# State space of a two-layer hybrid model: blocks of 32 partitions change places by ScalarE copies in place of products with columns of the identity

## The chip, the cores and the metric

The kernel runs on one core of a Trainium2 chip, one launch for the whole model. The metric is the device time of one execution in microseconds (us). The engines that matter here are TensorE (PE in the rows; PEld is its weight load), VectorE (DVE), ScalarE (ACT), and SyncE (SP), whose queue issues the weight transfers. Matrix products end in PSUM, eight banks of 2 KB per partition; all else lies in SBUF, on 128 partitions.

## The reference, cut to what matters

Two layers, 256 tokens, width 1024. Each layer adds a gated mixer of three branches (attention, state space, convolution) and then a feed-forward part: dense in layer 0, eight experts with two chosen per token in layer 1.

```python
for layer in range(2):
    h = rmsnorm(x, norm_mix[layer])
    z = h @ w_in[layer]
    cq, ckv, kpe, u_ssm, conv_a, conv_g, gates = split(z)
    y_attn = mla_branch(cq, ckv, kpe, ...) @ w_o_attn[layer]
    s = s5_branch(u_ssm, ...)
    s = gelu(s)
    s = s * sigmoid(s @ ssm_w_glu[layer] + ssm_b_glu[layer])
    y_ssm = s @ w_o_ssm[layer]
    y_conv = conformer_conv_branch(conv_a, conv_g, ...) @ w_o_conv[layer]
    g = sigmoid(gates).reshape(B, L, 3, D)
    x = x + (g[:, :, 0] * y_attn + g[:, :, 1] * y_ssm + g[:, :, 2] * y_conv) @ w_out[layer]
    x = x + (swiglu if layer == 0 else moe_swiglu)(rmsnorm(x, norm_ffn[layer]), ...)
return rmsnorm(x, norm_final)

# s5_branch, for each of 32 groups of 16 channels with 64 complex states:
#   state[t] = a * state[t-1] + B u[t];   y[t] = Re(C state[t]) + d * u[t]
```

The state space is 512 channels wide: 32 groups of 16.

## The kernel before

The whole is one program whose instructions a scheduler orders on PE, ACT, DVE and SP by their dependencies and buffers, starting from the order in which the program emits them. A plan per layer lists the weight pieces of the mixer ("u0", "gate4", "conv1", ...); after each piece the "lanes", generators such as the state space's `ssm_gen`, are advanced by a budget of estimated microseconds. Those estimates are the numbers that the lanes yield. So the state space's small steps lie between the products of the projections, and a step that becomes ready late delays whatever stands behind it on the same engine.

**Projections.** A weight piece of 128x1024 arrives in fp32. ACT writes its rounded high part (`bwh`, L198), DVE the remainder (`bwl`, L199), and PE makes three products of high and low parts per tile (L211 to L213, helper `mm3`). Three pairs of `bwh`/`bwl` buffers are in turn. In layer 0 the product with `ssm_w_glu` is made in plain fp32 instead (L209).

**State space.** `u`, the branch's input, holds channels on partitions and tokens along the row: four tiles of 128 channels x 256 tokens. The scan goes in steps of Q = 4 tokens, so that a sequence is NQ = 64 blocks of 4. For this, `U` holds, for each of 16 pairs of groups, 32 channels times 4 time steps on the 128 partitions and 64 blocks along the row. The work is done in two halves h of 8 pairs each:

- `states(h)` brings `u` to `U`: 16 products per half (4 blocks of 32 channels r, 4 steps st; L1225), each with 32 columns of the identity as weights and `tile_position` set, take partitions 32r.. of `u`, every fourth token, to partitions 32(3-st).. of a PSUM tile `aux`. ACT copies the bank to `U` (L1228, 128x512). 16 fp32 products with `minT` (L1232) then give `bu`.
- `turn_in`, `scans`, `turn_out` are DVE work: rotate by the tables `E`, 16 scans of 64 (L1270), rotate back into `P0` and `P1` (`hr`, `hi`), which have one buffer each.
- `out(h)` makes 8 times three products into the one `y` bank (L1241 with `toep` and `U`; L1242 with `mout` and `P0`; L1243 with `P1`), and ACT copies the bank to `ys` (L1245, 128x512).
- `ssm_act(h)` brings `ys` back to channels on partitions by 16 products per half with identity columns (L1315, into `aux`); DVE adds d times `u` (two instructions through the helper at L136, which read `aux` with a stride of 64 elements). ACT squares (L1322), DVE combines, ACT takes the tanh (L1324), DVE writes the gelu into `u`; then comes the product with `ssm_w_glu`, in layer 1 after a split of `u` into `br` (L201, L202).

The mixer's PSUM tiles are `mm` (two banks), `bu` (two), and one each of `aux`, `y`, `sc` and `o`. `aux` also serves attention's norms and transposes and the convolution's norm. An fp32 product runs through PE in two passes, so 16 products show as x32 in the trace.

Of the kernel before, what the change touches and what calls it, by code (L numbers as in the profile page):

```python
# [8 lines left out]
F32 = mybir.dt.float32  # L9
F32R = mybir.dt.float32r  # L10
I32 = mybir.dt.int32
AF = mybir.ActivationFunctionType
OP = mybir.AluOpType
# [10 lines left out]
Q = 4  # L24
NQ = L // Q
# [33 lines left out]
def pair_at(c):  # L59

    h, r, q = c // 8, c // 2 % 4, c % 2
    return 4 * (2 * h + q) + r
# [19 lines left out]
class Prog:  # L82
# [43 lines left out]
    def tt(self, out, a, b, op):  # L126
        self.nc.vector.tensor_tensor(out, a, b, op=op)
# [743 lines left out]
    def mixer(self, l, wk, psp, raw=None):  # L871
        nc, io = self.nc, self.io
# [18 lines left out]
        aux = lambda: psp.tile([128, 512], F32, name="aux", bufs=1)  # L891
# [64 lines left out]
        u = wk.tile([128, 4, L], F32, name="u", bufs=1)  # L956
# [5 lines left out]
        def pair(user):  # L962

            t = wk.tile([128, 2, 4, L], F32R, name="br", bufs=2)
            return (t[:, 0].bitcast(F32), None) if user in nat else (t[:, 0], t[:, 1])
# [247 lines left out]
        def ssm_gen():  # L1213
            E = self.E
            U = wk.tile([128, NCH, NQ], F32, name="U", bufs=1)
            wt = lambda nm: wk.tile([128, 8, NQ], F32, tag=nm, name=nm, bufs=1)

            def states(h):

                p = aux()  # L1220
                us = u[:, 2 * h:2 * h + 2].rearrange("p q (k s) -> p s q k", s=Q)
                for r in range(4):
                    for st in range(Q):
                        o = 32 * (Q - 1 - st)
                        nc.tensor.matmul(p[o:o + 32, r * 128:(r + 1) * 128],  # L1225
                                         self.ident[:, 32 * r:32 * r + 32], us[:, st],
                                         start=True, stop=True, tile_position=(0, o))
                nc.scalar.activation(U[:, 8 * h:8 * h + 8].rearrange("p a b -> p (a b)"), p, AF.Copy)  # L1228
                pb = psp.tile([128, 2, 8, NQ], F32, name="bu", bufs=1)
                for i in range(2):  # L1230
                    for c in range(8):
                        nc.tensor.matmul(pb[:, i, c], self.minT[i][:, pair_at(8 * h + c)], U[:, 8 * h + c],  # L1232
                                         start=True, stop=True)
                return pb

            def out(h, hr, hi):
                y = psp.tile([128, 8, NQ], F32, name="y", bufs=1)
                mo = lambda i, c: self.mout[i][:, pair_at(c)].rearrange("p k g o -> p (k g o)")
                for j in range(8):
                    c = 8 * h + j  # L1240
                    nc.tensor.matmul(y[:, j], self.toep[:, pair_at(c)], U[:, c], start=True, stop=False)  # L1241
                    nc.tensor.matmul(y[:, j, 1:], mo(0, c), hr[:, j, :NQ - 1], start=False, stop=False)  # L1242
                    nc.tensor.matmul(y[:, j, 1:], mo(1, c), hi[:, j, :NQ - 1], start=False, stop=True)  # L1243
                Y = wk.tile([128, 8, NQ], F32, tag="ys", name="ys", bufs=1)
                nc.scalar.activation(Y, y, AF.Copy)  # L1245
                return Y

            tt = lambda o, x, y, op: self.tt(o, x, y, op)

            def turn_in(h, pb, wr, wi):  # L1250

                pr, pi = pb[:, 0], pb[:, 1]
                C, S = (E[:, i, 8 * h:8 * h + 8] for i in range(2))
                t = wt("T0")
                tt(wr, pr, C, OP.mult)
                tt(t, pi, S, OP.mult)
                yield 1.2
                tt(wr, wr, t, OP.add)
                t = wt("T0")
                tt(wi, pi, C, OP.mult)  # L1260
                yield 1.2
                tt(t, pr, S, OP.mult)
                tt(wi, wi, t, OP.subtract)
                yield 1.2

            def scans(h, wr, wi):
                for w_ in (wr, wi):
                    for c in range(8):
                        k = 16 * l + pair_at(8 * h + c)
                        nc.vector.tensor_tensor_scan(w_[:, c], self.magq[:, k:k + 1].to_broadcast([128, NQ]), w_[:, c],  # L1270
                                                     0.0, op0=OP.mult, op1=OP.add)
                    yield 1.1

            def turn_out(h, wr, wi):

                C, S = (E[:, i, 8 * h:8 * h + 8] for i in range(2))
                hr, hi, t = wt("P0"), wt("P1"), wt("T0")
                tt(hr, wr, C, OP.mult)
                tt(t, wi, S, OP.mult)
                yield 1.2  # L1280
                tt(hr, hr, t, OP.subtract)
                tt(hi, wr, S, OP.mult)
                yield 1.2
                tt(wi, wi, C, OP.mult)
                tt(hi, hi, wi, OP.add)
                yield 1.2
                return out(h, hr, hi)

            w = [wt("wr"), wt("wi")]
            pb = states(0)  # L1290
            yield 0
            yield from turn_in(0, pb, *w)
            pb = states(1)
            sg["states"] = True
            yield from scans(0, *w)
            Y = yield from turn_out(0, *w)
            w = [wt("wr"), wt("wi")]
            yield from turn_in(1, pb, *w)
            ssm_act(0, Y)
            yield 2.2  # L1300
            yield from scans(1, *w)
            Y = yield from turn_out(1, *w)
            yield 0
            ssm_act(1, Y)
            yield 2.2

        def ssm_act(h, Y):

            if h == 0:
                sg["H"], sg["L"] = pair("glu")  # L1310
            p = aux()
            pv = p.rearrange("p (q s k) -> p q s k", q=2, s=Q)
            for r in range(4):
                for st in range(Q):
                    nc.tensor.matmul(pv[32 * r:32 * r + 32, :, st], self.ident[:, 32 * st:32 * st + 32],  # L1315
                                     Y[:, 2 * r:2 * r + 2], start=True, stop=True, tile_position=(0, 32 * r))
            for q in range(2):
                yv = u[:, 2 * h + q].rearrange("p (k s) -> p k s", s=Q)
                self.stt(yv, yv, self.f("ssm_d", l, 2 * h + q), pv[:, q].rearrange("p s k -> p k s"), OP.mult, OP.add)
            y = u[:, 2 * h:2 * h + 2].rearrange("p a b -> p (a b)")  # L1320
            t = wk.tile([128, 512], F32, tag="T1", name="lt", bufs=1)
            nc.scalar.activation(t, y, AF.Square, scale=math.sqrt(0.044715))  # L1322
            self.stt(t, t, 1.0, y, OP.add, OP.mult)
            nc.scalar.activation(t, t, AF.Tanh, scale=math.sqrt(2.0 / math.pi))  # L1324
            self.stt(y, t, 1.0, y, OP.add, OP.mult)
            if sg["L"] is not None:
                fl = lambda v: v[:, 2 * h:2 * h + 2].rearrange("p a b -> p (a b)")
                self.split(fl(sg["H"]), fl(sg["L"]), y, scale=0.5)
# [25 lines left out]
        if l == 0:  # L1354
            self.conv_params(psp)
        lanes = dict(tables=lambda: self.ssm_tables(l), out=lambda: self.ssm_out(l, psp),
                     norm=attn_norm, attn=attn_gen, ssm=ssm_gen, cln=conv_ln)
        lanes["in"] = lambda: self.ssm_inp(l, psp)
        needs = dict(ssm=("tables", "out", "in"), attn=("norm",), cln=("conv0", "conv1"))
        needs["in"] = ("out", "attn") if l == 0 else ()  # L1360
        for tok in self.plan[l]:
# [6 lines left out]
            name, i = t[:-1], int(t[-1], 16)  # L1368
# [621 lines left out]
```

## Time and profile before

| | |
|---|---|
| time, median of 3 runs | 1738.11 us (1738.04 to 1740.32) |
| the profiled execution's own time | 1739.71 us |
| its span in the profile | 1738.0 us |
| PE busy | 1696.0 us (98%) |
| DVE busy | 1473.3 us (85%) |
| ACT busy | 1164.1 us (67%) |
| chain that ended last | PE 92%, DVE 4%, ACT 2%, issue 1%, DMA 1% |
| mean granted TensorE clock | 0.992 |

The span is first to last instruction. The granted clock is the share of TensorE's full speed that the chip allowed. Layer 0's mixer lies in about the first 200 us of the span, its dense feed-forward part up to about 490, layer 1's mixer from there to about 740, and the experts fill the rest. In rows of the trace the columns are start, duration, engine, line, operation, output <- inputs, partitions x elements, and, in brackets, how long the engine was idle before and what ended that.

### The profile page before, as it was taken

What the parts mean: (1) busy time and instruction counts of PE and PEld (TensorE: products, weight loads), DVE (VectorE), ACT (ScalarE), POOL (GpSimd) and SP (SyncE); (2) the same over time, 40 slices, a digit from 0 to 9 for tenths busy, and PEclk for the clock granted to TensorE, in tenths of its full rate; (3) what the DMA queues carried; (4) which work ended last, traced back from release to release, by engine and by line L of the source; (5) the groups of instructions that cost most, each with busy time, mean ns of one, the idle gap of its engine ahead of it and who ended that gap; (6) DMA issues with size and microseconds to landing.
All of it is one profiled execution on the core that took longest, in us unless ns stands there. A gap on an engine that the chain in (4) does not pass through costs nothing.

```text
span 1738.0 us, 26083 instructions
## 1 busy us (share of the span) xinstructions
PE 1696.0 (98%) x9705; PEld 1461.0 (84%) x9705; DVE 1473.3 (85%) x2170; ACT 1164.1 (67%) x1519; POOL 41.5 (2%) x64
## 2 busy tenths in 40 slices
PE   7999999999999999999999999999999999999996
PEld 6899898999999898888888888888788888888875
DVE  7888987845579898789999999898898988989897
ACT  4645555654444465567887887787877887878775
POOL 2000000000000000000000000000000000000020
PEclk9999999999999899989999999999999999999999
DMA  5523355645545646679999799699999899898993
GB/s 156 152 80 99 121 178 175 180 154 194 179 137 164 222 155 218 236 254 386 359 368 396 278 380 396 250 394 395 341 393 393 307 394 388 336 394 319 395 394 137
DMA packets 262311, 471.27 MB, mean 271 GB/s; under 512 B 26832, under 2 KB 104816, under 8 KB 262176
## 3 DMA queue, kind: packets, MB, share of 16 engines
q1 hardware_dynamic: 245124, 455.70, 72.9%
q10 hardware_dynamic: 14732, 5.79, 1.3%
q0 software_dynamic: 2320, 8.03, 1.2%
q8 instruction: 78, 1.28, 0.3%
q14 instruction: 57, 0.47, 0.1%
HBM read 463.70 MB, written 5.78 MB: 270 GB/s over the span
## 4 chain that ended last, share of the span: by engine, by line
PE 92%; DVE 4%; ACT 2%; issue 1%; DMA 1%; ACTq 0%; DVEq 0%
PE mm L212 19%; PE mm L211 19%; PE mm L213 19%; PE Y L212 6%; PE Y L213 6%; PE Y L211 6%; PE acc L213 2%; PE acc L212 2%; PE acc L211 2%; PE tr L1784 1%; PE mm L209 1%; DVE bwl L199 1%; PE bu L1232 1%; PE spare L629 1%; ACT bwh L198 1%
## 5 line engine op out<-in xcount | busy, mean ns | idle before, releaser
L198 ACT ACTIVATE bwh<-braw 128x1024 fp32r<-128x1024 f32 x248 | 261.0, 1058 | 207.2 <-PE mm L212 129.4
L199 DVE TENSOR_TENSOR bwl<-braw,bwh 128x1024 fp32r<-128x1024 f32 x248 | 301.1, 1222 | 98.4 <-ACT bwh L198 93.1
L211 PE MATMUL mm<-bwh,bxm 128*128 128x512 f32 x672 | 266.5, 397 | 0.0
L212 PE MATMUL mm<-bwl,bxm 128*128 128x512 f32 x672 | 265.0, 394 | 1.2 <-DVE bwl L199 1.2
L213 PE MATMUL mm<-bwh,bxm 128*128 128x512 f32 x672 | 263.0, 391 | 0.0
L211 PE MATMUL mm<-aH,bwh 128*128 128x256 f32 x544 | 157.7, 290 | 0.4 <-ACT bwh L198 0.3
L213 PE MATMUL mm<-aH,bwl 128*128 128x256 f32 x544 | 154.7, 284 | 1.6 <-DVE bwl L199 1.6
L212 PE MATMUL mm<-aL,bwh 128*128 128x256 f32 x544 | 154.9, 285 | 0.0
L212 PEld LDWEIGHTS mm<-bwl,bxm 128*128 128x128 f32 x672 | 126.4, 188 | 33.6 <-DVE bwl L199 9.4
L213 PEld LDWEIGHTS mm<-bwh,bxm 128*128 128x128 f32 x672 | 126.2, 188 | 25.8
L211 PEld LDWEIGHTS mm<-bwh,bxm 128*128 128x128 f32 x672 | 126.4, 188 | 25.2
L212 PE MATMUL Y<-bwl,bgates 128*128 128x512 f32 x336 | 133.7, 398 | 0.7 <-DVE bwl L199 0.7
L213 PE MATMUL Y<-bwh,bgates 128*128 128x512 f32 x336 | 132.9, 395 | 0.0
L211 PE MATMUL Y<-bwh,bgates 128*128 128x512 f32 x336 | 122.6, 400 | 0.0
L136 DVE SCALAR_TENSOR_TENSOR cacc<-zc,lc,cacc 128x256 f32<-128x256 f32 x240 | 108.5, 477 | 2.9 <-ACT cacc L1022 2.1
L211 PEld LDWEIGHTS mm<-aH,bwh 128*128 128x128 f32 x544 | 104.6, 192 | 3.8 <-issue 1.9
L213 PEld LDWEIGHTS mm<-aH,bwl 128*128 128x128 f32 x544 | 104.4, 192 | 2.1 <-DVE bwl L199 2.1
L212 PEld LDWEIGHTS mm<-aL,bwh 128*128 128x128 f32 x544 | 104.6, 192 | 0.3
L213 PE MATMUL mm<-fH,bwl 128*128 128x256 f32 x352 | 99.6, 283 | 0.2 <-DVE bwl L199 0.2
L212 PE MATMUL mm<-fL,bwh 128*128 128x256 f32 x352 | 99.5, 283 | 0.0
L211 PE MATMUL mm<-fH,bwh 128*128 128x256 f32 x352 | 99.4, 282 | 0.0
L213 PE MATMUL mm<-baH,bxm 128*128 128x512 f32 x224 | 87.8, 392 | 0.0
(427 smaller groups left out, 4189.5 us busy)
## 6 DMA issues: line engine op xcount, KB each, us to landing
bmout<-in_moe_w SPq DMA_DIRECT2D x46, 1024.0 KB, 10.7
bbr<-in_moe_w SPq DMA_DIRECT2D x44, 1024.0 KB, 12.6
braw<-in_moe_w SPq DMA_DIRECT2D x44, 1024.0 KB, 13.8
braw<-in_w_in SPq DMA_DIRECT2D x36, 1024.0 KB, 5.2
braw<-in_ffn_w SPq DMA_DIRECT2D x31, 1024.0 KB, 5.2
bE<-in_moe_w SPq DMA_DIRECT2D x23, 1024.0 KB, 10.5
btoep<-in_moe_w SPq DMA_DIRECT2D x23, 1024.0 KB, 11.6
bq<-in_moe_w SPq DMA_DIRECT2D x23, 1024.0 KB, 14.8
```

Source lines behind the costliest of these rows:

```text
L136: self.nc.vector.scalar_tensor_tensor(out, a, s, b, op0=op0, op1=op1)
L198: i = nc.scalar.activation(h, src, AF.Copy)
L199: j = nc.vector.tensor_tensor(l, src, h.bitcast(F32), op=OP.subtract)
L209: mm(out, wh, xh, start=start, stop=stop, skip_group_check=True)
L211: mm(out, wh, xh, start=start, stop=False, skip_group_check=True)
L212: mm(out, wh, xl, start=False, stop=False, skip_group_check=True)
L213: self.lastmm = mm(out, wl, xh, start=False, stop=stop, skip_group_check=True).ins
L629: nc.tensor.matmul(p[:, 32 * j:32 * j + 32], fx(self.bx[:, i, j]), c0m[:, i, 4 * u + j].rearrange("p a b -> p (a b)"), start=(i == 0), sto ...
L1232: nc.tensor.matmul(pb[:, i, c], self.minT[i][:, pair_at(8 * h + c)], U[:, 8 * h + c], start=True, stop=True)
L1784: nc.tensor.transpose(p[:, q * 128:(q + 1) * 128], s[:, q * 128:(q + 1) * 128], self.ident)
```

## The change

The identity products are gone from both places. `steps(h)` writes `U` by 16 ACT copies of 32 partitions x 128 elements (two pairs x 64 blocks, read from `u` with a stride of four elements); both halves' copies are emitted at the start, ahead of `states(0)`. `out(h)` writes `ys` by 16 ACT copies of 32x128 straight from the `y` bank, into a tile that now has channels on partitions and tokens in their order (written with a stride of four). DVE reads `ys` from SBUF, and `aux` is no longer used by the state space. Over both layers, 128 products (256 PE instructions in the trace) and 8 ACT copies of 128x512 go, and 128 ACT copies of 32x128 come.

```diff
-            def states(h):
-
-                p = aux()
+            def steps(h):
+
                 us = u[:, 2 * h:2 * h + 2].rearrange("p q (k s) -> p s q k", s=Q)
                 for r in range(4):
                     for st in range(Q):
                         o = 32 * (Q - 1 - st)
-                        nc.tensor.matmul(p[o:o + 32, r * 128:(r + 1) * 128],
-                                         self.ident[:, 32 * r:32 * r + 32], us[:, st],
-                                         start=True, stop=True, tile_position=(0, o))
-                nc.scalar.activation(U[:, 8 * h:8 * h + 8].rearrange("p a b -> p (a b)"), p, AF.Copy)
+                        c = 8 * h + 2 * r
+                        nc.scalar.activation(U[o:o + 32, c:c + 2], us[32 * r:32 * r + 32, st], AF.Copy)
+
+            def states(h):
+
                 pb = psp.tile([128, 2, 8, NQ], F32, name="bu", bufs=1)
...
-                Y = wk.tile([128, 8, NQ], F32, tag="ys", name="ys", bufs=1)
-                nc.scalar.activation(Y, y, AF.Copy)
+
+                Y = wk.tile([128, 2, NQ, Q], F32, tag="ys", name="ys", bufs=1)
+                for r in range(4):
+                    for st in range(Q):
+                        nc.scalar.activation(Y[32 * r:32 * r + 32, :, :, st], y[32 * st:32 * st + 32, 2 * r:2 * r + 2],
+                                             AF.Copy)
                 return Y
...
             w = [wt("wr"), wt("wi")]
+            steps(0)
+            yield 0
+            steps(1)
+            yield 0
             pb = states(0)
...
-            p = aux()
-            pv = p.rearrange("p (q s k) -> p q s k", q=2, s=Q)
-            for r in range(4):
-                for st in range(Q):
-                    nc.tensor.matmul(pv[32 * r:32 * r + 32, :, st], self.ident[:, 32 * st:32 * st + 32],
-                                     Y[:, 2 * r:2 * r + 2], start=True, stop=True, tile_position=(0, 32 * r))
             for q in range(2):
-                yv = u[:, 2 * h + q].rearrange("p (k s) -> p k s", s=Q)
-                self.stt(yv, yv, self.f("ssm_d", l, 2 * h + q), pv[:, q].rearrange("p s k -> p k s"), OP.mult, OP.add)
+                yv = u[:, 2 * h + q]
+                self.stt(yv, yv, self.f("ssm_d", l, 2 * h + q), Y[:, q].rearrange("p k s -> p (k s)"), OP.mult, OP.add)
```

The change also moves instructions on the engines, since the scheduler places the rest anew. In the changed kernel, lines from L1226 on have other numbers (Square is L1324, tanh L1326).

On ACT, at the start of layer 0's state space, the change places its copies for both halves like this (L637 expands the table `toep`, L1081 frees the `aux` bank for attention's norm):

```order
L1225 ACTIVATE U<-u 32x128
L637 ACTIVATE toep<-toep 32x16x32 x6
L198 ACTIVATE bwh<-braw 128x1024
L1225 ACTIVATE U<-u 32x128 x15
L925 ACTIVATE gates<-mm 128x512
L1225 ACTIVATE U<-u 32x128 x16
L1081 ACTIVATE cqk<-aux 64x256
```

What was one copy of 128x512 behind a `bwh`, and a second one 20 rows later, is now 32 copies in a row but for one instruction, with attention's L1081 behind them.

On DVE, in layer 0 between the first and the second half's outputs, the order was this (numbers tell buffers apart; `P0`, `P1` belong to the second half, `u` is the first half's skip term and then its gelu):

```order
L127 TENSOR_TENSOR P0_1602<-wr_1551,E_74 128x512
L127 TENSOR_TENSOR P1_1603<-wr_1551,E_74 128x512
L127 TENSOR_TENSOR P0_1602<-P0_1602,T0_1604 128x512
L127 TENSOR_TENSOR P1_1603<-P1_1603,wi_1552 128x512
L136 SCALAR_TENSOR_TENSOR u_365<-u_365,fv_108,aux_1562 128x256 x2
```

and in the changed kernel it is this:

```order
L127 TENSOR_TENSOR P0_1596<-wr_1562,E_74 128x512
L127 TENSOR_TENSOR T0_1598<-wi_1563,E_74 128x512
L127 TENSOR_TENSOR P1_1597<-wr_1562,E_74 128x512
L127 TENSOR_TENSOR P0_1596<-P0_1596,T0_1598 128x512
L136 SCALAR_TENSOR_TENSOR u_365<-u_365,fv_108,ys_1545 128x256 x2
L127 TENSOR_TENSOR wi_1563<-wi_1563,E_74 128x512
L1174 ISA sm_1834,st_1833<-sc_1830,lc_82 128x128
L1174 ISA st_1833 128x1
L136 SCALAR_TENSOR_TENSOR lt_1575<-lt_1575,u_365 128x512
L127 TENSOR_TENSOR P1_1597<-P1_1597,wi_1563 128x512
```

The last addition into `P1`, which the second half's products L1243 read, stood ahead of the two instructions on `u` and now stands behind them and behind the `lt` step, which reads ACT's Square.

On ACT, at the second half's output of layer 1, the order was

```order
L1245 ACTIVATE ys<-y 128x512
L198 ACTIVATE bwh<-braw 128x1024
L925 ACTIVATE gates<-gates 128x512
L1322 ACTIVATE lt<-u 128x512
L1081 ACTIVATE cqk<-aux 64x256
L1108 ACTIVATE k<-cqk 64x2048
L1324 ACTIVATE lt<-lt 128x512
L201 ACTIVATE br<-u 128x512
```

and is now

```order
L1248 ACTIVATE ys<-y 32x128 x16
L198 ACTIVATE bwh<-braw 128x1024
L925 ACTIVATE gates<-gates 128x512
L1081 ACTIVATE cqk<-aux 64x256
L1108 ACTIVATE k<-cqk 64x2048
L1324 ACTIVATE lt<-u 128x512
L1326 ACTIVATE lt<-lt 128x512
L201 ACTIVATE br<-u 128x512
```

The Square (now L1324) went behind attention's long L1108.

## Rows read from the trace of the kernel before

**Rows 1.** Busy time by stretch: length, then PE, PEld, DVE, ACT, POOL, clock, DMA, GB/s.

```profile
760.00:1738.00 978.00, 963.34 (x4327) 782.46 (x4325) 884.77 (x911) 766.65 (x862) 24.26 (x11) 1.00 0.94 354
```

**Rows 2.** Timeline of PE, layer 0, the first block of identity products (start, duration, engine).

```profile
89.34 2.02 PE L1225 MATMUL aux<-u,ident 128*32 128x128 f32 x32
...
91.52 0.28 PE L212 MATMUL mm<-aL,bwh 128*128 128x256 f32 x1
91.64 0.28 PE L213 MATMUL mm<-aH,bwl 128*128 128x256 f32 x1
```

**Rows 3.** Groups of ACT instructions by shape, whole span: busy, mean ns, idle before.

```profile
L619 ACT ACTIVATE bx<-ab 64x256 f32<-64x256 f32 x32 | 13.3, 415 | 12.0 <-DVE ab L127 5.9 <-PE spare L629 5.6
...
L632 ACT ACTIVATE toep<-spare 128x128 f32<-128x128 f32 x8 | 2.1, 262 | 2.5 <-PE spare L629 2.5
```

**Rows 4.** Timeline of ACT, layer 0: copies behind one another.

```profile
87.89 3.83 ACT L637 ACTIVATE toep<-toep 32x512 f32<-32x512 f32 x6
...
117.11 0.24 ACT L798 ACTIVATE braw<-braw 128x64 f32<-128x64 f32 x1
117.26 0.24 ACT L799 ACTIVATE braw<-braw 128x64 f32<-128x64 f32 x1
```

**Rows 5.** Timeline of PE, layer 0, between the two outputs of the state space.

```profile
151.53 0.39 PE L1243 MATMUL y<-P,mout 128*128 128x63 f32 x2
151.76 0.88 PE L1148 MATMUL sc<-k,q 128*128 128x128 f32 x4
152.61 2.46 PE L1315 MATMUL aux<-ys,ident 128*32 128x128 f32 x32
...
155.49 0.39 PE L1243 MATMUL y<-P,mout 128*128 128x63 f32 x2
```

**Rows 6.** Timeline of DVE, the same place.

```profile
151.74 1.29 DVE L127 TENSOR_TENSOR P<-wr,E 128x512 f32<-128x512 f32 x2 [0.47 <-PE y L1242]
...
153.55 0.68 DVE L127 TENSOR_TENSOR P<-P,wi 128x512 f32<-128x512 f32 x1
155.11 0.87 DVE L136 SCALAR_TENSOR_TENSOR u<-u,fv,aux 128x256 f32<-128x256 f32 x2 [0.87 <-PE aux L1315]
```

**Rows 7.** Timeline of ACT, the same place.

```profile
156.01 0.63 ACT L1322 ACTIVATE lt<-u 128x512 f32<-128x512 f32 x1 [3.46 <-DVE u L136]
```

**Rows 8.** Timeline of PE, layer 0, behind the second output.

```profile
160.18 0.39 PE L1243 MATMUL y<-P,mout 128*128 128x63 f32 x2
...
167.88 1.35 PE L209 MATMUL mm<-u,braw 128*128 128x256 f32 x5
```

**Rows 9.** Timeline of ACT, layer 1, around the first output.

```profile
532.17 0.60 ACT L1245 ACTIVATE ys<-y 128x512 f32<-128x512 f32 x1 [4.72 <-PE y L1243]
534.62 1.06 ACT L198 ACTIVATE bwh<-braw 128x1024 fp32r<-128x1024 f32 x1 [1.85 <-PE mm L212]
```

**Rows 10.** Timeline of PE, layer 1, behind the second output.

```profile
568.12 0.39 PE L1243 MATMUL y<-P,mout 128*128 128x63 f32 x2
...
571.15 0.28 PE L213 MATMUL mm<-aH,bwl 128*128 128x256 f32 x1
...
573.97 0.28 PE L212 MATMUL mm<-br,bwh 128*128 128x256 f32 x1
...
583.15 0.79 PE L211 MATMUL mm<-br,bwh 128*128 128x256 f32 x2 [3.44 <-ACT br L201]
```

**Rows 11.** Timeline of ACT, the same place.

```profile
577.96 1.91 ACT L1108 ACTIVATE k<-cqk 64x2048 f32<-64x2048 f32 x1
```

**Rows 12.** Busy time by stretch, layer 1, around that wait of PE.

```profile
579.00:581.00 2.00, 0.72 (x5) 0.63 (x4) 1.25 (x6) 1.50 (x2) 0.00 (x0) 0.52 1.04 387
...
587.00:589.00 2.00, 2.00 (x11) 2.00 (x11) 2.00 (x5) 1.55 (x4) 0.00 (x0) 0.50 0.01 4
```

**Rows 13.** Groups of DVE instructions by shape: busy, mean ns, idle before.

```profile
L136 DVE SCALAR_TENSOR_TENSOR cacc<-zc,lc,cacc 128x256 f32<-128x256 f32 x240 | 108.5, 477 | 2.9 <-ACT cacc L1022 2.1
...
L136 DVE SCALAR_TENSOR_TENSOR u<-u,fv,aux 128x256 f32<-128x256 f32 x8 | 3.5, 477 | 2.3 <-PE aux L1315 2.2
```

## The prediction

> **What bounds the kernel now.** I read the page's busy times and chain first: PE is busy for 98% of the span and makes 92% of the chain, so time is saved only where PE's work shrinks or PE waits less. The reader should then ask whether time saved in the mixers survives the experts, which fill the last 978 us. There PE is busy 963 us at clock 1.00, with the DMA engines at 0.94 [rows 1]. PE has no wait on a transfer in the stretch's groups, so I carry a shift of the mixers through to the end. The rest of the reading is local: the timeline of PE around each of the state space's eight places (input and output, two halves, two layers), then ACT and DVE at the same instants, to see who ends each wait.
>
> **Duration of one new copy.** No row shows 32x128 on ACT, so I bound it. From SBUF: six copies of 32x512 take 3.83 us, a step of 0.638 each, no overlap at all; the 64x256 group has a mean of 0.415 [rows 3, 4]. The difference over 256 elements gives 0.87 ns per element, so 128 elements cost 0.415 - 0.111 = 0.30 us, and 16 of them 4.9. From PSUM: 128x128 takes 0.262 [rows 3], with hardly a gap 0.27, so 16 take 4.3. The lower bound is the pair L798, L799: 0.24 long but 0.15 apart, an overlap of 0.09 [rows 4]. With it a copy costs 0.20 and a block of 16 about 3.2. I take the upper values, because the L637 copies, like the new ones, have 32 partitions and a start partition that changes from one to the next, and L798 and L799 have 128.
>
> **Inputs (`steps` for L1225).** A block of 32 instructions holds PE from 89.34 to the next ordinary product; 91.52 is one product step of 0.12 behind that, so it costs 2.18 - 0.12 = 2.06 [rows 2]. Two blocks per layer: 4.1 us off the path of PE in each layer, whether or not anything else waits. Against it: in layer 0 the copies for both halves stand on ACT ahead of L1081 (order above), so 32 x 0.30 = 9.7 us of ACT work is put before attention's norm; replayed along the new order, the `bu` products wait about 0.5 for `U` and the norm's products about 1.0 for the `aux` bank, 1.5 in all (bounds 0, if the projections cover it, and 4.9, one whole block). In layer 1 they stand between two `bwh`; I take 1.0 by the same replay. **Gain: 2.6 in layer 0, 3.1 in layer 1.**
>
> **First output of layer 0.** The first half's `y` products end at 151.53 + 0.39 = 151.92; the second half's first L1243 starts at 155.49, 3.57 later [rows 5]. L1315 took 2.46 of these, but DVE only gets to `P0` and `P1` at 151.74, since they have one buffer and wait for the first half's products, and the last addition into `P1` ends at 153.55 + 0.68 = 154.23 [rows 6]. So without L1315 and with nothing new, 155.49 - 154.3 = 1.2 could be won. But the new order puts the `P1` addition behind `u` and `lt`. Its chain from the end of the products: 16 copies 4.35, the two `u` 0.87 [rows 6], Square 0.63 [rows 7], `lt` and the addition 0.6 to 0.7 each like the 0.68 of `P` [rows 6], which makes 7.2. The second half starts 7.2 - 3.57 = **3.6 us later** than before. PE has only 0.88 of `sc` products [rows 5] and single `y` products to fill it: it idles some 3.6 us for the bank, then 2.6 for `P1`.
>
> **The clock there.** In layer 1 such a pause already exists: PE waits 3.44 before 583.15 [rows 10], the granted clock is 0.52 and 0.50 in the stretches shown and still 0.50 at 587 to 589 with PE fully busy [rows 12]. That is the lower level, 1.2 GHz. At half speed every us of PE work costs 0.5 more; from 583.15 to 589 that is 2.9. I expect the same fall in layer 0 behind the new pause, on products a part of which wait for other engines anyway: **2.2 lost**, bounds 0 and 2.9.
>
> **Second output of layer 0.** From the end of `y` at 160.57 to the second half's L209 products at 167.88 are 7.3 [rows 8], a chain through L1315, `u`, Square, `lt`, tanh and `u`, not PE's work. The new chain is 4.35 + 0.87 + 0.63 + 0.68 + 0.63 + 0.68 = 7.8, with hand-over gaps 8.2: 0.9 more. In the new order one more pair of `sc` products stands ahead of that wait (0.9 by [rows 5]), so it nets to **0**.
>
> **First output of layer 1.** L1315 leaves the path of PE; at the second output the same block costs 573.97 - 571.15 less two steps of 0.12, 2.58 [rows 10]. Against it, `y` ends about 532.15 and a `bwh` started at 534.62, 2.45 later [rows 9]; it now stands behind 16 copies, so it starts 1.9 later, and I let all of that through (bounds 0, if three buffers cover it, and 4.3). **Gain 0.7.** The two `u` steps on DVE also wait for the copies, with `bwl` and scans queued behind them; that is in the upper bound.
>
> **Second output of layer 1.** PE resumes at 583.15, 14.6 after `y` ends at 568.51; the chain went L1315, `u`, Square, L1108, tanh, `u`, `br` [rows 10]. Without L1315 the projections, the convolution's norm and L1081 move up 2.6, but Square now stands behind L1108 of 1.91 [rows 11], which eats part: Square 0.63 and its `lt` 0.68 lie behind it now and lay ahead before. 2.6 - 0.63 - 0.68 = 1.3; a lighter DVE queue may return 0.2. **Gain 1.5**, bounds 0 and 2.6. The pause stays, so the clock falls here as before.
>
> **Sum.** Layer 0: 2.6 - 3.6 - 2.2 + 0 = -3.2, that is slower. Layer 1: 3.1 + 0.7 + 1.5 = +5.3. Net 2.1 us less, so the profiled execution of 1739.71 becomes 1737.6. Its time is 1.60 above the median of the runs, 1738.11, so I forecast **1736.0 us**. A measurement can tell about 0.2% from no change, 3.5 us here: below 1734.6 is faster, above 1741.6 slower.
>
> **Rivals.**
> 1. *The clock holds in layer 0.* PE's pause is split by some `y` products, and the trace shows no pause of this pattern. Then the 2.2 are not lost: 1733.8. Against it: rows 12 show a fall after pauses of this size.
> 2. *The copies overlap* by 0.09, as L798 and L799 do [rows 4]: a block takes 3.2, so 1.1 comes back at layer 0's first output, 0.9 at its second, 1.1 at layer 1's first and about 1.6 of the 2.5 lost to the inputs; 4.7 in sum, 1731.3, and 1729.1 if the clock holds too. The Trainium skill has this as a rule (ScalarE: Activation LUTs, section What ACT_TABLE_LOAD costs): an ACTIVATE with immediate operands costs 186 ns plus 0.833 ns per element, and those back to back overlap by about 93 ns. By it alone a copy would be 0.20. The trace agrees for the 128-partition pair and not for the six 32-partition copies.
> 3. *Slower: the stride doubles the element time.* Each new copy reads or writes every fourth fp32 element in SBUF. If an element then takes twice as long, that is 0.11 more per copy, 1.8 per block, and it falls on the chains that end in PE: both outputs of layer 0, the first of layer 1, and one block of each layer's inputs, 5 x 1.8 = 9.0, so 1745.0. It decides from about 0.07 per copy (5.6 in the sum). The rows nearest speak against it: DVE's `u` with a strided operand takes 477 ns, just as `cacc` without one [rows 13]; none shows ACT. The Trainium skill (SBUF — State Buffer, section Door 1: The DMA port swizzle, note on cachelines) says that SBUF has lines of 16 bytes and that each access crossing to a new line pays a penalty; four fp32 elements apart, each access does.
>
> **How the numbers follow.** The forecast has 0.42, with a range of its own of 1732.5 to 1739.5 from the terms' bounds; two thirds of it lie within 0.2% of before. The clock that holds has 0.18, the overlap 0.13, the stride 0.09. The last 0.18 are terms at their bad ends (the whole 4.3 of layer 1's first output or the 4.9 of the inputs lost), 1738 to 1744. That sums to faster 0.38 (0.12 + 0.11 + 0.13 + 0.02), same 0.42 (0.27 + 0.07 + 0.08), slower 0.20 (0.03 + 0.09 + 0.08). The range of 1729 to 1744 leaves out the overlap with the clock held, in part, and the stride.
>
> **What would show it.** Right: U copies of 0.30 and `ys` copies of 0.27, each starting when the last ends; PE idle twice between the two outputs of layer 0, the second time for DVE's `P`; granted clock near 0.50 right behind; layer 1's wait for `br` some 1.5 earlier after `y`. Wrong: steps of 0.20 or of 0.40 per copy; a first L1243 of the second half less than 5 us after the first half's end; clock 1.00 there; or a `bwh` in layer 1 that holds up PE by more than 2 us.

## The result, and the profile after

The changed kernel takes 1767.64 us (median of 4 runs, 1764.61 to 1773.32) against 1738.07 before: a ratio of 1.0169, 95% interval 1.0155 to 1.0184. It is 29.6 us slower, where 1736.0 had been forecast and a range up to 1744. The profiled execution is the longest of the four, 1773.32, with a span of 1771.6.

Where the time went is read from instructions that both kernels have. From one-line views of the kernel before: L1051 (the convolution's activation), L948 (start of layer 1).

```profile
L1051 ACT ACTIVATE lt<-cacc,fvh x8: 496/497/511, 239.4 to 698.2; 128x256 f32<-128x256 f32 x8
L948 ACT ACTIVATE R<-aux x1: 365/365/365, 498.3 to 498.3; 128x256 f32<-128x256 f32 x1
```

The same of the changed kernel; the times behind the durations are first and last start.

```profile
L1051 ACT ACTIVATE lt<-cacc,fvh x8: 492/494/511, 262.4 to 731.6; 128x256 f32<-128x256 f32 x8
L948 ACT ACTIVATE R<-aux x1: 364/364/364, 525.4 to 525.4; 128x256 f32<-128x256 f32 x1
```

Of the 33.6 us between the two spans, 23.0 arise up to the convolution's activation in layer 0's mixer (239.4 to 262.4; the mixer reaches past that point, not only to about 200), 4.1 more up to layer 1, and 6.5 in layer 1. The stretch around the state space tells what kind of time it is; in the changed kernel it begins 1.3 later, for a reason given below. Busy time by stretch, before (length, PE, PEld, DVE, ACT, POOL, clock, DMA, GB/s):

```profile
85.00:239.40 154.40, 153.47 (x1222) 141.07 (x1221) 129.50 (x325) 78.58 (x153) 4.25 (x8) 1.00 0.37 113
```

and after:

```profile
86.30:262.40 176.10, 160.81 (x1094) 147.57 (x1093) 129.69 (x325) 102.77 (x213) 4.25 (x8) 0.89 0.33 99
85.00:125.00 40.00, 36.30 (x231) 33.65 (x231) 22.97 (x54) 28.86 (x61) 0.00 (x0) 0.87 0.29 83
150.00:200.00 50.00, 39.32 (x202) 34.02 (x201) 31.07 (x100) 28.00 (x73) 4.25 (x8) 0.73 0.11 31
370.00:380.00 10.00, 10.00 (x43) 9.33 (x42) 5.41 (x9) 4.93 (x10) 0.00 (x0) 0.52 0.31 103
```

PE is idle for 15.3 us instead of 0.9. It is also busy for 7.3 us longer, although the products that were removed had held it for about 9 (two blocks of 2.06 and two of 2.46). So the same work took some 16 us longer, at a granted clock of 0.87 and 0.73 in stretches that had 1.00. The 21.7 us of this stretch are thus 14.4 of new waits and some 16 of lower clock, less the 9 of removed products. The clock fell once more at 370 to 380, in the dense feed-forward part; that answers to most of the 4.1.

Two of the falls stand where both kernels do the same. PE's first 463 instructions are the same in both. At 55 to 75, where it waits for `bwl` in either kernel, they show this, first before, then after:

```profile
61.73 0.39 PE L213 MATMUL mm<-aH,bwl 128*128 128x256 f32 x1 [1.60 <-DVE bwl L199]
55.00:75.00 20.00, 18.01 (x114) 15.90 (x114) 18.50 (x37) 11.25 (x21) 0.00 (x0) 1.00 0.54 139
61.73 0.39 PE L213 MATMUL mm<-aH,bwl 128*128 128x256 f32 x1 [1.51 <-DVE bwl L199]
55.00:75.00 20.00, 17.84 (x103) 15.93 (x102) 18.50 (x37) 10.70 (x20) 0.00 (x0) 0.91 0.57 140
```

The clock fell behind the same wait in one execution and not in the other, and it cost 1.3 us ahead of the state space. Of the 14 traces here that share these 463 instructions, 8 have this fall and 6 have not. The fall at 370 is alike: PE waits 0.76 for `minT` shortly before it (366.49), and as long in the kernel before (343.63), where no fall follows. So some 5 of the 33.6 us are the chance of the profiled execution, which is 5.7 above the median.

For the whole span PE's line of the page after is this:

```profile
PE 1705.4 (96%) x9449; PEld 1469.7 (83%) x9449; DVE 1472.8 (83%) x2170; ACT 1212.1 (68%) x1639; POOL 41.5 (2%) x64
```

PE's idle time went from 42.0 (1738.0 less 1696.0) to 66.2. Its busy time rose by 9.4, although some 18 us of products are gone. By this estimate, from busy times alone, the 33.6 are 24 of waits and 27 of lower clock, less 18.

The new copies, from the timeline of ACT after (start, duration, engine; x15 is fifteen copies in a row):

```profile
94.46 6.65 ACT L1225 ACTIVATE U<-u 32x128 f32<-32x128 f32 x15
...
101.60 7.05 ACT L1225 ACTIVATE U<-u 32x128 f32<-32x128 f32 x16
108.67 0.38 ACT L1081 ACTIVATE cqk<-aux 64x256 f32<-64x256 f32 x1
...
158.62 6.37 ACT L1248 ACTIVATE ys<-y 32x128 f32<-32x128 f32 x16 [6.80 <-PE y L1243]
```

A copy steps by 0.44 from SBUF and 0.40 from PSUM, where [rows 3, 4] had given 0.30 and 0.27. Between the two outputs of layer 0, the place of [rows 5], PE shows this:

```profile
158.20 0.39 PE L1243 MATMUL y<-P,mout 128*128 128x63 f32 x2
158.42 0.88 PE L1148 MATMUL sc<-k,q 128*128 128x128 f32 x4
165.05 0.69 PE L1241 MATMUL y<-U,toep 128*128 128x64 f32 x2 [5.75 <-ACT ys L1248]
...
167.98 0.69 PE L1243 MATMUL y<-P,mout 128*128 128x63 f32 x2 [1.82 <-DVE P L127]
```

and DVE, the place of [rows 6]:

```profile
165.03 0.88 DVE L136 SCALAR_TENSOR_TENSOR u<-u,fv,ys 128x256 f32<-128x256 f32 x2 [4.13 <-ACT ys L1248]
...
167.24 0.69 DVE L127 TENSOR_TENSOR P<-P,wi 128x512 f32<-128x512 f32 x1
```

The reader should see the forecast chain link by link: 16 copies, then `u`, Square, `lt`, and only then `P`. It takes 9.4 us from 158.59 to 167.98, not 7.2, of which the copies are 6.4 instead of 4.35, and the bank and `P1` are the two waits foretold. What follows, `y` products of 0.63 to 0.69 per pair instead of 0.39, is the lower level of the clock.

### The profile page after: what moved, and what is told of

Its sections match the earlier page's. It is cut to its first block, busy times and chain, and to the rows that moved or that the text cites. A ratio compares the mean times of both kernels' runs of the same rounds, so it can differ in the third digit from the quotient of the medians.

```text
span 1771.6 us, 25699 instructions
## 1 busy us (share of the span) xinstructions
PE 1705.4 (96%) x9449; PEld 1469.7 (83%) x9449; DVE 1472.8 (83%) x2170; ACT 1212.1 (68%) x1639; POOL 41.5 (2%) x64
## 4 chain that ended last, share of the span: by engine, by line
PE 87%; ACT 5%; DVE 5%; issue 1%; DMA 1%; ACTq 0%; DVEq 0%
PE mm L212 18%; PE mm L211 18%; PE mm L213 18%; PE Y L212 6%; PE Y L213 6%; PE Y L211 6%; PE acc L213 2%; PE acc L212 2%; PE acc L211 2%; PE mm L209 1%; PE tr L1786 1%; ACT ys L1248 1%; DVE bwl L199 1%; ACT bwh L198 1%; ACT U L1225 1%
## 5 line engine op out<-in xcount | busy, mean ns | idle before, releaser
L212 PEld LDWEIGHTS mm<-bwl,bxm 128*128 128x128 f32 x672 | 126.3, 188 | 33.6 <-DVE bwl L199 9.4
```

The lines of the kernel that those rows point to most:

```text
L212: mm(out, wh, xl, start=False, stop=False, skip_group_check=True)
```

## The experiments

**The parts alone.** Inputs by copies with outputs as before, and the reverse:

```diff
 steps_only: identity products into U removed, + steps(0), steps(1); identity products of L1315 kept
 outs_only:  identity products into U kept; + 16 copies y -> ys, identity products of L1315 removed
```

> Only the inputs by ScalarE copies, the outputs as before. Theory (PE waits for the copies, and the clock falls behind each longer wait): in the changed kernel's trace the inputs of layer 0 show some 3.6 us of new PE waits and about 4.7 us lost at the lower clock against 4.1 us of removed products, layer 1 about 2.7 and 3.4 against 4.1; so 6 us slower, 1744 (1740 to 1749). Rival (nearly all of the loss is the outputs'): 1732 to 1738, the removed products won.

> Only the outputs by ScalarE copies, the inputs as before. Theory: the larger part of the 29.6 us, 17 to 25 us slower, 1755 to 1763, with the two long pauses of PE in layer 0 and a granted clock of 0.50 from the first of them to the glu products. Rival (the two parts make each other worse, so that neither alone is bad): under 1748.

Measured: inputs alone 1753.32, ratio 1.0079 (1.0057 to 1.0102), 13 us; outputs alone 1760.95, 1.0123 (1.0103 to 1.0142), 21 us, against 1740.26 on that chip. Both are bad alone, and their sum, 34, is somewhat over the whole, 29.6: the rival in which one part carries all of it falls, and so does the one in which neither alone is bad. The inputs cost twice what I expected. Busy time by stretch of the run with inputs alone:

```profile
85.00:125.00 40.00, 37.54 (x258) 35.49 (x257) 26.08 (x64) 31.05 (x66) 0.00 (x0) 0.91 0.31 87
150.00:180.00 30.00, 27.15 (x192) 23.61 (x191) 18.66 (x61) 7.97 (x19) 4.24 (x8) 0.83 0.13 37
```

The second stretch lies some 40 us behind the copies, at the outputs, which this kernel makes as before. The moved order of DVE (skip term ahead of the additions into `P`) is there too, with two PE waits for `P` of 1.20 and 1.37, and the clock falls behind them.

**What makes a copy dear.**

```diff
-    nc.scalar.activation(U[o:o + 32, c:c + 2], us[32 * r:32 * r + 32, st], AF.Copy)
+    # one line for each kind: u2[.., 64*st:64*st+64], [.., a+b:a+128:2], us[.., st], 128 in a row
```

> The changed kernel with other data in its copies, the same 32x128 each, one line of the kernel per kind; which channels and tokens the state space gets is thereby changed. Inputs, SBUF to SBUF: rows of 64 without a stride, a stride of two elements, of four (as in the change), and 128 elements in one row. Outputs, PSUM to SBUF: written in one row, with a stride of two, of four, and as in the change. Theory (an element that does not share its 16 bytes with the one before costs twice): without a stride 0.30 and 0.27, stride two the same or little more, stride four 0.43 and 0.39. Rival 1 (any stride costs): stride two as dear as four. Rival 2 (the cost is one of 32 partitions): all alike, 0.43.

Groups of ACT instructions by shape of that run (busy, mean ns); in the kernel's order L1225 has no stride, L1227 two, L1229 four, L1231 one row; on the outputs L1256 no stride, L1258 two, L1259 four, L1260 as in the change.

```profile
L1229 ACT ACTIVATE U<-u 32x128 f32<-32x128 f32 x16 | 6.8, 428 | 0.2
L1260 ACT ACTIVATE ys<-y 32x128 f32<-32x128 f32 x16 | 6.2, 390 | 0.2
L1259 ACT ACTIVATE ys<-y 32x128 f32<-32x128 f32 x16 | 6.2, 390 | 0.2
L1227 ACT ACTIVATE U<-u 32x128 f32<-32x128 f32 x16 | 5.0, 315 | 0.3
L1225 ACT ACTIVATE U<-u 32x128 f32<-32x128 f32 x16 | 4.9, 308 | 1.8 <-DVE u L127 1.6
L1231 ACT ACTIVATE U<-u 32x128 f32<-32x128 f32 x16 | 4.9, 307 | 0.2
L1258 ACT ACTIVATE ys<-y 32x128 f32<-32x128 f32 x16 | 4.5, 278 | 0.2
L1256 ACT ACTIVATE ys<-y 32x128 f32<-32x128 f32 x16 | 4.3, 269 | 24.2 <-PE y L1250 24.0
```

A stride of two fp32 elements adds 7 to 9 ns, a stride of four 120 ns, 0.94 per element, read or written in SBUF. That is what the theory expects, and both rivals fall; strides of three or eight were not run. The Trainium skill (SBUF — State Buffer, section Door 1: The DMA port swizzle, note on cachelines) says that lines are of 16 bytes and that every access which crosses to a new one pays; ScalarE's copies agree: two elements to such a line cost 7 to 9 ns more than four, one to a line 120 ns more.

**Outputs written without the stride.** ys in rows of 64, the stride moved to DVE's read:

```diff
...
-    Y[32 * r:32 * r + 32, :, :, st]
+    Y[32 * r:32 * r + 32, :, st]          # tile [128, 2, Q, NQ]; read as "p s k -> p k s"
...
```

> The changed kernel with ys written in rows of 64 (no stride on the write); VectorE reads it with a stride instead. Theory (the stride costs a copy its additional 0.12 us): the copies step by about 0.27 instead of 0.40, the outputs' chains in layer 0 are 2 us shorter each, the pauses and the low clock shorter: 1755 to 1763. Rival (the cost is one of 32 partitions or of the instruction): step still 0.40 and the time 1764 to 1770.

1755.00, ratio 1.0087 (1.0069 to 1.0104), copies of 268 ns. 64 copies shorter by 0.12, 7.7 us of ACT work in all, gave about 14 us of time, the lower edge of the theory's range. The profiled executions are 18.1 apart: PE idles 7.1 us less (59.1 against 66.2) and is busy 11.0 less with the same products, as less of its work lies in the lower clock; some 5 of that are the chance falls of the changed kernel's profile. So the gain is larger than the waits that went. The stride was not free on VectorE either. Its `u` steps, after the change and in this run (busy, mean ns):

```profile
L136 DVE SCALAR_TENSOR_TENSOR u<-u,fv,ys 128x256 f32<-128x256 f32 x8 | 3.6, 481 | 12.7 <-ACT ys L1248 12.7
L136 DVE SCALAR_TENSOR_TENSOR u<-u,fv,ys 128x256 f32<-128x256 f32 x8 | 5.1, 671 | 7.1 <-ACT ys L1248 7.1
```

**The order on VectorE.** The addition into `P1` ahead of the skip term in layer 0:

```diff
+                if h and l == 0:
+                    ssm_act(0, Y0[0])
...
+            with (self.tc.issue_after(sg["add"]) if h == 0 and l == 0 else ExitStack()):   # sg["add"]: the addition into P1
...
```

> The changed kernel, but in layer 0 VectorE makes the last addition into P1 before the skip term of the first half. Theory (behind the copies, the second half's products wait for P1 as well): they start when the y bank is free, 6.5 us after the first half's instead of some 9.5, and the time falls by 3 to 6, 1762 to 1765. Rival (the bank alone sets it, or the later skip term costs the same): 1766 to 1769.

1766.30, 1.0158 (1.0141 to 1.0175), and 1.0165 (1.0151 to 1.0179) in a second run. The addition moved as foretold: the second half's first L1243 starts 7.4 us after the first half's end (163.95 after 156.54) instead of 9.4, and PE no longer waits for `P1` there. But against 1.0169 that is no measurable gain; the expectation failed. PE waits again behind the second output for the convolution's norm (2.5), for `sm` (1.5) and for `pts` (0.8), all behind the copies on ACT.

**Filling PE's pauses.** Products of 128x512 in fp32 (0.87 each) into a bank that nothing reads, behind layer 0's outputs: 7 and 7, then 10 and 7.

```diff
+            if l == 0:
+                f = mmt().rearrange("p a b -> p (a b)")
+                for _ in range((7, 7)[h]):
+                    nc.tensor.matmul(f, self.ident, self.E.rearrange("p a b c -> p (a b c)")[:, :512],
+                                     start=True, stop=True)
```

> The changed kernel with seven products of 128x512 in fp32 (about 6 us) added behind each of layer 0's two outputs, into a bank that nothing reads. Theory (the lower clock behind PE's pauses costs more than the pauses' own end): PE is busy through the pauses, the granted clock stays at 1.00 between the outputs, and in spite of 12 us of added work the kernel is 4 to 12 us faster than the changed one: 1756 to 1763. Rival (the clock follows something else, or what waits is what counts): as slow as the changed kernel or slower, 1767 to 1780.

> As the run with seven added products behind each output, but ten behind the first, since with seven PE still waited 2.5 us for P1 and the clock fell. Theory (PE's pause is what lets the clock fall): three more products (2.6 us of work), yet the clock stays near 1.00 from 150 to 200 and the kernel is 2 to 8 us faster than with seven: 1761 to 1767. Rival (added work counts as such): 1771 to 1774.

1769.38, 1.0177 (1.0160 to 1.0194), and 1771.11, 1.0176 (1.0157 to 1.0195): as slow as the changed kernel, so both expectations failed. Work of 12 and 15 us was added at almost no cost, but PE still waited for `P1` behind the filling (2.5 and 0.7), and the clock still fell: at 150 to 200 it is 0.86 and 0.93, against 0.73 in the changed kernel. These runs don't settle what the clock costs. Therefore one pause alone, beside the same kernel without it:

> The changed kernel with the last addition into P1 of layer 0 ahead of the skip term, again, beside the next run on the same chip: 1.0158 of before as in its first run (1.0145 to 1.0170); PE waits 5.8 us for the y bank and works at half clock behind it.

> The same with six products of 128x512 in fp32 (5.2 us) added in that one pause of PE, into a bank that nothing reads; the second half's products then wait for nothing else. Theory (the pause itself costs nothing that could be saved there, but the fall of the clock behind it does): clock 1.00 through 150 to 180, the second half's y products take 5.4 us instead of 9.4, and the kernel is 3 to 6 us faster than the run beside it although PE does more. Rival (the lower clock lies on work that waits for other engines anyway): no faster, within 1.5 us of it, or slower.

1767.10 without, 1763.00 (1.0143, 1.0127 to 1.0158) with six products. Busy time by stretch, without them:

```profile
155.00:180.00 25.00, 15.27 (x67) 13.99 (x66) 10.86 (x33) 16.08 (x43) 4.25 (x8) 0.73 0.12 34
```

and with them:

```profile
155.00:180.00 25.00, 20.08 (x84) 15.49 (x84) 13.96 (x43) 17.84 (x46) 4.24 (x8) 0.79 0.11 31
```

The second half's `y` products take 8.5 us (160.62 to the next product at 169.09) instead of 10.3 (160.83 to 171.12), not the 5.4 expected, and the clock is not 1.00: it came down later, PE having waited 1.4 behind the filling. The kernel is 4.1 us faster by the medians, as expected, with 5.2 us more work. But the intervals overlap by a hair, and the two profiled executions took 1761.77 and 1761.49: in them the six products fill 5.3 us of PE's idle time (64.3 to 59.0) and no time is gained. The mean granted clock of the executions, 0.976 to 0.982 without and 0.979 to 0.983 with, fits the theory. So the direction is likely, not certain.

**Copies where nobody waits.** U in a buffer of its own, filled right behind the projection of u; then also the order on VectorE mended:

```diff
             nc.scalar.activation(u[:, 2 * i:2 * i + 2], p, AF.Copy)
+            steps(i)
```

> Outputs as before; the input copies are issued right behind the projection of u, into a buffer of their own, so that U is there long before it is used (in layer 0). Theory (a copy costs only where PE waits for it): PE loses 4.1 us of work in layer 0 and waits for nothing new there; in layer 1 the copies lie directly ahead of their use and may cost what they save: 1731 to 1736. Rival (64 copies cost ACT 27 us, and the splits of the weights come late): 1738 to 1745.

> Outputs by products as before, input copies right behind the projection of u, and in layer 0 the last addition into P1 before the skip term. Theory (the loss of the run with early copies alone came of that order on VectorE, and of the lower clock behind it): the waits of y for P in layer 0 go, and the clock stays up at 150 to 180: 1738 to 1745. Rival (the weight splits behind the blocks of copies are the loss): 1748 to 1753.

1751.95 (1.0083, 1.0052 to 1.0115) and 1749.60 (1.0070, 1.0053 to 1.0087). By time the two can't be told apart. The traces tell more: in the second run the waits of the `y` products for `P` are 0.8 instead of 2.6, the granted clock is 1.00 from 150 to 180, and layer 0's L1051 instruction (L1053 there) comes at 243.9 instead of 248.9. PE's idle time up to there fell by only 0.9 (20.4 to 19.5), so most of the 5.0 is clock. But both are slower than forecast, and the reason is the rival's. Timeline of ACT of the second run:

```profile
24.42 7.04 ACT L1219 ACTIVATE U<-u 32x128 f32<-32x128 f32 x16
31.49 2.00 ACT L198 ACTIVATE bwh<-braw 128x1024 fp32r<-128x1024 f32 x2
```

A block of 16 copies holds up the weight splits, PE waits 3.23 for one of them, and the clock falls at 30 to 40. There a product that started at 35.7 before starts at 42.6, 6.9 of the 8.5 us by which layer 1 begins later (506.8 against 498.3).

**All strides off ScalarE.** u kept in the order of blocks, its skip term written over U, ys in rows, the order mended:

> The changed kernel with all 128 copies free of strides (u is kept in the order of the blocks and its skip term is written over U, ys in rows, the strides are VectorE's and the projection's) and the last addition into P1 before the skip term in layer 0. Theory (the stride is the first cause, the waits for blocks of 16 copies the second): copies of 0.31 and 0.27, 1744 to 1751, still slower than before. Rival (with copies of the length I had forecast the forecast was right): 1732 to 1740.

1752.05, 1.0067 (1.0048 to 1.0086), just above what I expected, with copies of 308 and 268 ns. So with copies of just the length that I forecast the kernel is still some 12 us slower: the forecast would have failed without the stride too, though VectorE's eight `u` steps, which have the strides now, take 680 ns here instead of 481. PE waits 3.8 for the bank at the first output of layer 0, and the clock is 0.77 from 150 to 180.

**Only where it pays.** Copies for layer 1's inputs alone, then the same with u laid out for copies without a stride:

```diff
+            if l:
+                steps(0)
...
+                steps(1)
...
```

> The change in one place only: layer 1's inputs by copies, all else as before. In the run with inputs alone, the stretch from the start of layer 1 to the end was 1.5 us shorter than before. Theory (there the copies cost less than the products): 1735 to 1738. Rival (a clock fall takes its place): 1740 to 1745.

> As layer 1's inputs by copies, with u laid out so that the copies read rows of 64 without a stride: 0.31 each instead of 0.43, so the bu products wait some 2 us less: 1733 to 1737, faster than before if anything is. Rival (the waits are for the weight splits behind the copies, not for the copies): as the run with strided copies.

1741.21, 1.0004 (0.9995 to 1.0012): no change. 1737.42, 0.9987 (0.9977 to 0.9996), against 1739.93 on that chip: the only version here that is faster than both kernels, by about 0.13%, which the interval barely tells from none. Waits of PE with the strided copies (total, times, longest):

```profile
PE bu L1242 <- ACT U L1225: 2.7, 3, 1.2
```

and without the stride:

```profile
PE bu L1250 <- ACT U L1233: 0.7, 1, 0.7
```

The reader should not give all of the 3.8 us between these two to the stride. PE's instructions in layer 0 are the same in both and in the kernel before, yet in the profiled executions layer 1 starts at 502.2 with the strided copies, at 499.0 without the stride and at 498.3 before. With the strided copies the clock fell three times in layer 0 behind waits that the others have as well:

```profile
55.00:75.00 20.00, 18.11 (x106) 16.20 (x104) 18.75 (x37) 10.98 (x20) 0.00 (x0) 0.91 0.54 135
295.00:315.00 20.00, 17.83 (x127) 17.16 (x127) 15.83 (x18) 12.30 (x16) 0.00 (x0) 0.91 0.46 146
340.00:360.00 20.00, 19.18 (x137) 17.90 (x135) 16.54 (x45) 13.12 (x23) 0.00 (x0) 0.91 0.42 147
```

From the start of layer 1 to the end the three take 1238.4, 1236.7 and 1239.7 us. One trace each does not make more of it than this: in layer 1 the copies seem to save 1 to 3 us.

## Why the prediction was wrong

- **Carried right.** The removed products, the order on DVE, the wait for the bank, the wait for `P1`, the fall of the clock behind them and the place of each were as forecast. Nothing in the experts' stretch gave the loss back.
- **"Duration of one new copy" failed first.** I took 0.30 and 0.27 from rows without a stride and put the doubled element into rival 3 at 9 in 100. It measured 0.44 and 0.40, slightly over that rival's price of 0.11 more. The row that I held against it, DVE's `u` at 477 ns [rows 13], reads its strided operand `aux` from PSUM; with the strided operand in SBUF the same instruction takes 671 (ys_rows). The first output's chain became 9.4 instead of 7.2, the inputs' blocks 7.0 instead of 4.9. By ys_rows this term is worth about 14 us on the outputs.
- **"The clock there" failed most.** I allowed one fall, worth 2.2 and at most 2.9. The mixer of layer 0 alone lost some 16 us of PE time to it: at 103 to 117 behind the waits for `U` and `aux`, from 161 to 181, and again from 185. I had limited it by the part of one existing fall in which PE was busy [rows 12]. What should have been asked at each new wait is whether the clock falls there. Even the waits for `U`, of about 1.1 each, and in steps_only those for `P`, had a fall behind them. But a wait of this size is no sure sign: behind the same waits for `U` in layer 1 (1.07 and 1.21) the clock fell in the changed kernel and stayed up in order_filler, as it did behind the 1.60 for `bwl` before.
- **Rival 3's sum, 1745.0, was too low for the same reason.** It added the copies' lengths along the chains and nothing for the clock; the range ended at 1744.
- **"Second output of layer 0 nets to 0" failed.** From the end of `y` to the glu products at the place of [rows 8] it was 12.2 (177.63 to 189.83) against 8.2 forecast. The copies themselves make 2.0 of the difference. The attention's steps behind 16 copies on ACT, which I left out, held up the products that were to fill the wait.
- **Layer 1 had the wrong sign.** I forecast 5.3 gained; the profiled execution lost 6.5. At the inputs the `bu` products wait 2.7 for `U` where 1.0 had been allowed. The second output, the place of [rows 10 and 11], shows it:

```profile
608.14 2.64 PE L750 MATMUL aux<-ones,sq 128*128 128x1 f32 x12 [2.15 <-ACT cqk L1081]
615.54 0.80 PE L211 MATMUL mm<-br,bwh 128*128 128x256 f32 x2 [4.76 <-ACT br L201]
```

PE resumes 16.0 us after the end of `y` at 599.57, not 14.6 as before and not 13.1 as forecast. L1081, which I let move up by 2.6, now stands behind the copies and with it the long L1108. At the first output `bwh` starts 6.5 after `y` (571.14 after 564.59), so 4.1 late, not 1.9, of which PE waited 0.6 (for `bwl`, before 573.51).
- **Not settled:** what of the clock's share a kernel without the new waits would get back. The 16 us in layer 0's mixer and the 27 over the span are read from busy times of one execution, some 5 of them are chance, filling one pause moved 4.1 us by the medians, and no run here kept the clock up through all of the pauses.

## What to carry to other kernels

TensorE is the bottleneck here, and still a product that only moves data was cheap on it: moving a block of 16 to ScalarE took 2.1 to 2.5 us of work away and put 6.4 to 7.1 us (4.3 to 4.9 without a stride) into a queue on which weight splits, softmax steps and bank releases stand behind it. Price a new operation from a row with the same engine, the same memory and the same stride, and at every new wait of TensorE add the work behind it at the lower clock as a cost that some executions pay and others don't. Copies that remain should read and write SBUF with a stride of at most two fp32 elements. That they should stand where their block fits between two weight splits is a guess; no run here tried it. And before a difference of a few us between two traces is explained, look whether it lies where the kernels differ.

## What the runs showed of the hardware that was not expected

- ScalarE, 32x128 in fp32: 308 ns without a stride, 315 with a stride of two elements, 428 with four (SBUF read); 269, 278 and 390 when the write is strided.
- VectorE, SCALAR_TENSOR_TENSOR 128x256 in fp32: 477 ns with a strided operand read from PSUM [rows 13], 671 with one read from SBUF (ys_rows), 481 with all operands in order (after).
- Copies whose start partition changes did not overlap at all: 16 of about 0.43 us took 7.05. The Trainium skill (ScalarE: Activation LUTs, section What ACT_TABLE_LOAD costs) gives about 93 ns of overlap for instructions back to back; these runs show none for them.
- PE pauses of 5.8 and 1.8 us in a stretch were followed by the lower clock until 181, 13 us behind the second one, with PE busy throughout.
- The clock does not fall alike in each execution of the same instructions: behind PE's wait of 1.5 to 1.9 us for `bwl` at about 60, in an unchanged stretch, it fell in 8 traces of 14, after waits of 1.50 and of 1.86 and not after others of 1.47 and of 1.85.
